# The skip weights of the Mamba layer: one load of a table of 128 rows in place of two loads by single elements

## The chip, the cores and the metric

The kernel runs on one core of a Trainium2 chip. A core has a matrix engine (TensorE, PE in the profile; PEld is its loading of weights), three engines for elementwise work (VectorE or DVE, ScalarE or ACT, GpSimd or POOL), and SyncE (SP), which here only issues transfers. Sixteen DMA engines carry the transfers between the device memory (HBM) and the on-chip memory (SBUF, 128 partitions); PSUM takes the results of matrix products. The engines work side by side and wait for each other by semaphores. The metric is device time in microseconds of one execution; less is better. Outputs must agree with the reference.

## The reference

Two layers on 1024 latent tokens and 256 context tokens of width 1024: a Mamba layer (state space, both directions of time), then attention, each with a modulated norm before and a gate behind. Cut to what matters here:

```
for i in range(2):
    sh, scl, gt = split(silu(c) @ mod_w[i] + mod_b[i], 3)      # the same with c_ctx for the context tokens
    in_lat = rmsnorm(h_lat, norm_w[i]) * (1 + scl) + sh
    ...
# the Mamba layer
z, xbc, dt = split(h @ in_w);  xbc = silu(conv5(xbc) + conv_b)
xs, B, C = split(xbc);         dt = softplus(dt + dt_bias)
y = scan_forward(xs, dt, B, C) + scan_backward(...)            # 32 heads of 64 channels
y = y + dsk * xs                                               # dsk: one skip weight for each of the 32 heads
out = rmsnorm(y * silu(z), norm_w) @ out_w
```

The skip weights are the input m_d, 32 numbers. Shift and scale of the first layer come from the product of silu(c) and silu(c_ctx) with the first 2048 columns of mod_w[0].

## The kernel before, in words

Everything is float32; large products are made from a high and a low part of each operand, three matrix instructions per product (the helper mm3, lines 167 to 170).

**Who decides the order.** The kernel first makes a list of operations, each with an engine, a duration that was written in by hand, a rank, the operations it comes after and the buffers it takes. The class Plan then walks through these in a small event loop of its own (method order, lines 82 to 131). For each engine that is free it takes the operation of lowest rank whose predecessors are done and whose buffers are free. The result is one fixed order per engine, and the instructions are written in it. Transfers are operations of "SP": each keeps SP for 0.38 units of the list's time, and those made by the helper small (line 280) count as 0.05 of transfer time, the 256 KB pieces as 0.9. These are numbers of the list, not of the chip. The chip then runs each engine's instructions in that order, each as soon as its semaphores allow.

**The head.** Before the first large product the kernel does the following.

- It loads the 10 token tiles of 128 x 1024 (function normalised, line 339 for the load, 512 KB each, ranks from -1000 to -851). ScalarE squares and sums a tile, VectorE and GpSimd form the inverse root, VectorE scales the tile (line 353).
- It computes shift and scale of the first layer (function sums, lines 283 to 330). mod_w[0] comes in 32 pieces of 128 x 512 (256 KB, line 297, ranks -900 to -869) into a buffer named spare that holds 20 of them; a piece waits until the product twenty pieces earlier is done. Each piece is multiplied with cc, the 16 columns of silu(c) and silu(c_ctx) (line 303; two matrix instructions for each piece). Pieces 0 to 7 add into the PSUM tile st, 8 to 15 into yo, and the last sixteen into two yd tiles. ScalarE copies each sum out (mrow, line 313), TensorE turns it (line 319), and VectorE makes the columns shcol and gcol (lines 223 to 326).
- Function modulated (lines 356 to 379) turns the scaled tiles on TensorE, applies scale and shift (raw, lines 371 and 373) and splits them into the two parts inh and inl. All later products of the Mamba layer read these.
- Seven small loads are listed under the name rest (lines 397 to 400), with ranks -850 to -844: convw, convb, dtbias, a_bc, mnw, and two for dskip. Their sizes in SBUF are 128 x 160, 128 x 32, 64 x 1, 128 x 64, 128 x 16 and, for dskip, two times 64 x 16. (modbc of 128 x 32 and normw and cc of 128 x 16 are loaded at the start.)
- w_dt (256 KB, line 423) and the first halves of the projection weights w_in (256 KB each, line 606) follow with ranks of -30 and above, through two raw buffers (wraw). ScalarE makes their high part (lines 431 and 611), VectorE or GpSimd the low part (lines 434 and 614).

All these loads are issued by SP, on one queue, in the order of the list.

**The skip weights.** dskip is a tile of 128 partitions x 16 (line 248). Column j belongs to channel tile j of 128 channels, that is two heads: partitions 0 to 63 hold the weight of head 2j, partitions 64 to 127 that of head 2j + 1. m_d lies in HBM as 32 numbers in a row. Each of the two loads fills 64 partitions: all 64 read the same 16 numbers, every second one of m_d, from the first or the second on. The tile is read at line 822 alone, where VectorE adds skip weight times xs to the result of the scan.

**Behind the head** come the projections with their convolutions (lines 622 to 675), the scan by groups of heads (mix, from line 677), the gated norm and the output product, and the attention layer. TensorE's products set their pace.

Of the kernel before, what the change touches and what calls it, by code (L numbers as in the profile page):

```python
# [137 lines left out]
def rows(ap, parts):  # L138
    return bass.AP(tensor=ap.tensor, offset=ap.offset, ap=[[0, parts]] + [list(d) for d in ap.ap])
# [6 lines left out]
def emit(tc, A, out):  # L146
# [7 lines left out]
    def scratch(name, shape):  # L154
        return DR.tile(shape, FT, name=name)
# [8 lines left out]
    m_d = scratch("m_d", [2, 4096])  # L164
# [40 lines left out]
    convw = P0.tile([128, 32, 5], FT, name="convw")  # L205
    convb = P0.tile([128, 32], FT, name="convb")
    mnw = P0.tile([128, 16], FT, name="mnw")
# [40 lines left out]
    dskip = SM.tile([128, 16], FT, name="dskip")  # L248
    dtb = SM.tile([128, 1], FT, name="dtbias")
    dtbias = dtb[64:128]  # L250
    a_bc = SM.tile([128, 64], FT, name="a_bc")
# [28 lines left out]
    def small(rank, dst, src):  # L280
        return plan.op("SP", lambda: Q.dma_start(dst, src), [], rank, small=True)
# [112 lines left out]
    for b in range(3):  # L394
        modulated(b, xs[(0, 2, 6)[b]:(2, 6, 10)[b]], cols, -800 + 100 * b)

    rest = [small(-850 + i, *p) for i, p in enumerate(
        [(convw, A["conv_w"]), (convb, A["conv_b"]), (dtbias, A["dt_bias"]), (a_bc, rows(A["a_log"], 128)), (mnw, A["m_norm_w"])] +
        [(dskip[j * 64:(j + 1) * 64], bass.AP(tensor=A["m_d"].tensor, offset=A["m_d"].offset + j, ap=[[0, 64], [2, 16]]))
         for j in range(2)])]  # L400


    second = [plan.op("-", change("su2", reuse_waits="tile"), list(ready_in.values()), us=0.)]
# [1456 lines left out]
def layout(inp):  # L1860
    import numpy as np
    f=lambda n: np.asarray(inp[n])
    d = {}
    d['x']=f('x')[0]; d['ctx']=f('ctx')[0]
    cols=lambda v: v.reshape(-1,128).T
    d['cc']=np.stack([cols(f('c')[0]), cols(f('c_ctx'))],-1)
    d['norm_w']=np.stack([cols(f('norm_w')[i]) for i in range(2)],1)
    d['mod_w']=f('mod_w'); d['mod_b']=f('mod_b')
    d['mod_bc']=np.stack([cols(f('mod_b')[i][:2048]) for i in range(2)],1)
    d['final_norm_w']=f('final_norm_w')  # L1870
    w=f('m_in_w')[0]
    d['w_in']=w[:,:6144].reshape(8,128,48,128).transpose(2,1,0,3).reshape(48,128,1024)
    d['w_dt']=w[:,6144:].reshape(8,128,64).transpose(1,0,2).reshape(128,512)
    d['conv_w']=f('m_conv_w')[0].reshape(5,32,128).transpose(2,1,0)
    d['conv_b']=cols(f('m_conv_b')[0])
    d['a_log']=f('m_a_log')[0].reshape(64); d['dt_bias']=f('m_dt_bias')[0].reshape(64,1)
    d['m_d']=f('m_d')[0]
    d['m_norm_w']=cols(f('m_norm_w')[0])
    d['m_out_w']=f('m_out_w')[0]
    a=f('a_in_w')[0]  # L1880
    tile4=lambda w: w.reshape(8,128,512).transpose(1,0,2).reshape(128,4096)
    d['wqkv']=np.stack([tile4(a[:,j*512:(j+1)*512]) for j in range(3)])
    d['wg']=a[:,1536:].reshape(8,128,8,128).transpose(2,1,0,3).reshape(8,128,1024)
    d['a_out_w']=f('a_out_w')[0]
    d['q_norm']=f('a_q_norm')[0]; d['k_norm']=f('a_k_norm')[0]
    r,c=np.meshgrid(np.arange(16),np.arange(64),indexing='ij')
    inv=(np.float32(10000.0)**(-np.arange(0,32,2,dtype=np.float32)/np.float32(32))).astype(np.float32)
    ar=r.reshape(-1).astype(np.float32)[:,None]*inv; ac=c.reshape(-1).astype(np.float32)[:,None]*inv

    ang=np.stack([ar,ac],1)  # L1890
    cs=np.cos(ang); sn=np.sin(ang)
    cos=np.stack([cs,cs],2).reshape(1024,64); sin=np.stack([-sn,sn],2).reshape(1024,64)
    d['rope']=np.stack([cos,sin],1).reshape(8,128,2,64).transpose(1,0,2,3)
    return {k:np.ascontiguousarray(v,dtype=np.float32) for k,v in d.items()}
# [17 lines left out]
```

## Time and profile before

| | us |
|---|---|
| time, median of 3 runs | 1996.26 |
| lowest and highest | 1993.16, 1997.48 |
| profiled execution: span from first to last instruction | 1992.2 |
| TensorE busy in that span | 1923.3 (97%) |
| VectorE, ScalarE, GpSimd busy | 1450.7, 1114.1, 1199.4 |
| mean granted clock of TensorE | 0.989 of full speed |

For the profiled execution only the span is given, no time of its own beside it. Durations and starts are in microseconds from the span's start unless a row says ns. A row of a timeline gives start, duration, engine, line, operation, output<-inputs, shapes and count; brackets give the idle time just before it and who ended it. SPq is the issuing of a transfer by SP. The timeline merges neighbours of one kind, so that "x5" may contain waits. A row of waits gives who waited for whom: total, times, longest. The DMA share is a mean over the sixteen engines, and can come out a few per cent above 1.

### The profile page before, as it was taken

To read this page: it belongs to the slowest core of one execution; us is meant where nothing else is said; L and a number is where in the kernel's file an instruction comes from. 1 tells how busy PE (TensorE), PEld (TensorE's weight loads), DVE (VectorE), ACT (ScalarE), POOL (GpSimd) and SP (SyncE) were. 2 spreads that over 40 slices of the span, in tenths; PEclk is the share of its full clock that TensorE was granted. 3 is DMA by queue.
4 is the path that set the end of the run, shared out by engine and by line. 5 is a ranking of instruction groups with operands and counts; after the bars stand their busy time and mean duration, and the time that the engine had idled before them with its cause. 6 is when DMAs were issued, how large, how long until landed. Compare 5 with 4: busy or idle time off the path is not lost.

```text
span 1992.2 us, 30263 instructions
## 1 busy us (share of the span) xinstructions
PE 1923.3 (97%) x10552; PEld 1448.4 (73%) x10552; DVE 1450.7 (73%) x1734; ACT 1114.1 (56%) x2046; POOL 1199.4 (60%) x973
## 2 busy tenths in 40 slices
PE   5799999999999999999999999999999999999998
PEld 1578888888888888888878878877775444444476
DVE  1585887887969796867545898768675888888643
ACT  2537768666667777677644775533224454444521
POOL 1212766676757585768379788764355677776722
PEclk8899999999999999999999999999999999999999
DMA  6114463635363545356586675552232011110033
GB/s 246 64 32 131 129 187 115 186 104 174 115 190 104 149 137 175 121 151 175 162 278 206 224 253 187 165 152 93 77 109 83 32 39 48 48 46 24 9 104 106
DMA packets 162125, 255.48 MB, mean 128 GB/s; under 512 B 21466, under 2 KB 57178, under 8 KB 161972
## 3 DMA queue, kind: packets, MB, share of 16 engines
q1 hardware_dynamic: 160820, 251.71, 41.1%
q8 instruction: 83, 1.36, 0.3%
q10 hardware_dynamic: 1152, 1.84, 0.3%
q14 instruction: 70, 0.57, 0.1%
HBM read 210.78 MB, written 42.63 MB: 127 GB/s over the span
## 4 chain that ended last, share of the span: by engine, by line
PE 85%; DVE 6%; DMA 2%; issue 2%; ACT 2%; POOL 2%; SPq 1%; DVEq 0%; POOLq 0%; ACTq 0%
PE pj L168 10%; PE pj L169 10%; PE pj L170 10%; PE sc L1675 7%; PE ot L1691 7%; PE ob L168 7%; PE ob L170 6%; PE ob L169 6%; PE yo L849 3%; PE st L730 3%; PE sc L1474 2%; DVE acc L657 2%; PE yd L807 2%; PE sc L168 2%; PE sc L170 2%
## 5 line engine op out<-in xcount | busy, mean ns | idle before, releaser
L168 PE MATMUL pj<-inh,whi 128*128 128x512 f32 (+1 forms) x1152 | 442.0, 384 | 5.1 <-DVE dv L465 3.2
L169 PE MATMUL pj<-inl,whi 128*128 128x512 f32 (+1 forms) x1152 | 410.1, 356 | 0.8 <-POOL inl L379 0.8
L170 PE MATMUL pj<-inh,wlo 128*128 128x512 f32 (+1 forms) x1152 | 410.4, 356 | 0.0
L168 PEld LDWEIGHTS pj<-inh,whi 128*128 128x128 f32 x1152 | 219.1, 190 | 34.4 <-DVE dv L465 3.6
L170 PEld LDWEIGHTS pj<-inh,wlo 128*128 128x128 f32 x1152 | 218.2, 189 | 32.1
L169 PEld LDWEIGHTS pj<-inl,whi 128*128 128x128 f32 x1152 | 219.3, 190 | 26.9 <-POOL inl L379 1.2
L657 DVE SCALAR_TENSOR_TENSOR acc<-ub,convw,acc 128x1282 f32<-128x1282 f32 x128 | 229.2, 1791 | 10.5 <-ACT acc L654 6.4
L766 POOL TENSOR_SCALAR_AFFINE_SELECT lab<-lab 128x512 f32<-128x512 f32 x160 | 148.6, 934 | 143.0 <-DMA lab<-la_d 117.6
L772 ACT ACTIVATE W<-lab,u_t 128x128 f32<-128x128 f32 x640 | 203.4, 391 | 51.6 <-POOL lab L766 23.0
L1656 POOL TENSOR_TENSOR acc<-acc,P 128x1024 f32<-128x1024 f32 x80 | 192.5, 2406 | 64.5 <-ACT P L1680 62.9
L1680 ACT ACTIVATE P<-sc 128x1024 f32<-128x1024 f32 x160 | 162.7, 1025 | 115.7 <-PE sc L1675 106.0
L1621 DVE TENSOR_REDUCE mx<-sc 128x2 f32<-128x1024 f32 (+1 forms) x140 | 167.4, 1214 | 38.6 <-PE sc L1474 37.6
L725 POOL TENSOR_TENSOR xw<-xst,te_t 128x256 f32<-128x256 f32 x144 | 145.9, 1026 | 27.6 <-PE st L730 17.8
L1691 PE MATMUL ot<-P,vv 128*64 128x512 f32 x640 | 154.7, 605 | 0.0
L614 POOL TENSOR_TENSOR wlo<-wraw,whi 128x512 fp32r<-128x512 f32 x48 | 70.9, 1477 | 122.8 <-ACT whi L611 119.1
L1675 PE MATMUL sc<-q,kh 64*128 64x512 f32 x640 | 135.9, 420 | 0.5 <-ACT P L1680 0.2
L785 DVE TENSOR_TENSOR W<-W 128x512 f32<-128x512 f32 x80 | 81.8, 1023 | 47.4 <-ACT W L772 42.4
L170 PE MATMUL ob<-whi,yl 128*128 128x512 f32 x288 | 113.4, 394 | 1.9 <-DVE yl L1073 1.4
L168 PE MATMUL ob<-whi,yh 128*128 128x512 f32 x288 | 113.9, 395 | 0.0
L169 PE MATMUL ob<-wlo,yh 128*128 128x512 f32 x288 | 112.9, 392 | 0.0
L1675 PEld LDWEIGHTS sc<-q,kh 64*128 64x128 f32 x640 | 60.0, 184 | 69.8 <-DVE mx L1621 29.6
L744 POOL TENSOR_TENSOR tm<-PV,dec_t 128x512 f32<-128x512 f32 x64 | 89.2, 1393 | 35.2 <-DVE PV L748 34.4
(285 smaller groups left out, 4446.1 us busy)
## 6 DMA issues: line engine op xcount, KB each, us to landing
lab<-la_d SPq DMA_DIRECT2D x160, 256.0 KB
wraw<-in_w_in SPq DMA_DIRECT2D x96, 256.0 KB
workvv<-in_m_out_w SPq DMA_DIRECT2D x94, 256.0 KB
mraw<-in_mod_w SPq DMA_DIRECT2D x64, 256.0 KB
es<-e_d SPq DMA_DIRECT2D x128, 128.0 KB
wraw<-in_wqkv SPq DMA_DIRECT2D x48, 256.0 KB
spare<-in_mod_w SPq DMA_DIRECT2D x32, 256.0 KB
q_d<-qs SPq DMA_DIRECT2D x64, 128.0 KB
```

What stands on the lines that cost most here:

```text
L168: T.matmul(o, lh, rh, start=first, stop=False)
L169: T.matmul(o, lh, rl, start=False, stop=False)
L170: T.matmul(o, ll, rh, start=False, stop=last)
L657: V.scalar_tensor_tensor(t["a"], ub[i % 2][:, k:k + CW], convw[:, ct, k:k + 1], t["a"], op0=OP.mult, op1=OP.add)
L725: G.tensor_tensor(t[d], s["xst"][:, c], te_t[:, d, c, h4][:, :, None].to_broadcast([128, 4, 64]), op=OP.mult)
L766: G.affine_select(t["l", d], t["l", d], [[0, 4], [sgn, 128]], OP.is_ge, NEVER, base=0, channel_multiplier=-sgn)
L772: S.activation(t["w", d][:, h], t["l", d][:, h], AF.Exp, bias=u_t[:, d, c, 4 * g + h:4 * g + h + 1])
L1621: V.tensor_reduce(max_place(t["m"][0], i), o, AX.X, OP.max)
L1656: E.tensor_tensor(t[e], t["P", k0] if two else t[e], t["P", kt], op=OP.add)
L1675: T.matmul(o[:, h], (first_row[r] if n == 3 else (kh, kl, kh)[n][r, kv, k]), x[(0, 0, 1, 2)[n]][r], start=(n == 0), stop=(n == 3))
L1680: S.activation(t["P", kt], flat(t["s", kt]), AF.Exp)
L1691: T.matmul(t["o"][h * 64:(h + 1) * 64], vv[:, kt, kv], t["P", kt][:, h * 512:(h + 1) * 512], start=(kt == 0), stop=(kt == NT - 1))
```

## The change

The host lays the skip weights out as the tile needs them: 128 rows of 16 numbers, each weight repeated over its 64 rows. The two entries for dskip in the list become one, a plain load of 128 x 16, of the same shape as mnw ahead of it. It has rank -845, which the first of the two had; rank -844 is gone, so the list has one SP operation fewer. Nothing else in the kernel is edited; the order is worked out anew from the list.

```
     rest = [small(-850 + i, *p) for i, p in enumerate(
-        [(convw, A["conv_w"]), (convb, A["conv_b"]), (dtbias, A["dt_bias"]), (a_bc, rows(A["a_log"], 128)), (mnw, A["m_norm_w"])] +
-        [(dskip[j * 64:(j + 1) * 64], bass.AP(tensor=A["m_d"].tensor, offset=A["m_d"].offset + j, ap=[[0, 64], [2, 16]]))
-         for j in range(2)])]
+        [(convw, A["conv_w"]), (convb, A["conv_b"]), (dtbias, A["dt_bias"]), (a_bc, rows(A["a_log"], 128)), (mnw, A["m_norm_w"]),
+         (dskip, A["m_d"])])]
...
-    d['m_d']=f('m_d')[0]
+    d['m_d']=np.repeat(f('m_d')[0].reshape(16,2).T,64,axis=0)
```

The function small is `plan.op("SP", lambda: Q.dma_start(dst, src), [], rank, small=True)`; layout, which holds the last two lines, runs on the host before the launch.

## The prediction

> **What bounds the kernel now.** I read the page first: the busy shares, then the slices, to find where TensorE isn't busy.
>
> ```profile
> span 1992.2 us, 30263 instructions
> PE 1923.3 (97%) x10552; PEld 1448.4 (73%) x10552; DVE 1450.7 (73%) x1734; ACT 1114.1 (56%) x2046; POOL 1199.4 (60%) x973
> PE   5799999999999999999999999999999999999998
> ```
>
> TensorE is busy 97% of the span, so for nearly all of it only TensorE's own work counts. The idle 68.9 us (1992.2 - 1923.3) are not spread evenly: only the first two slices (about 100 us) show a 5 and a 7. A change to a transfer of 4 KB can matter only there, since its data are first used at 215.5 us (the first issue of line 822, the only reader of the skip weights). The view of busy time by stretches cuts this head; its columns are the stretch, its length, the busy time of PE, PEld, DVE, ACT and POOL, then the granted clock, the DMA share and GB/s:
>
> ```profile
> core 0: us, PE busy (x) PEld busy (x) DVE busy (x) ACT busy (x) POOL busy (x), PEclk, DMA share, GB/s
> 5.00:35.00 30.00, 25.57 (x66) 5.32 (x66) 7.23 (x17) 11.88 (x21) 4.51 (x9) 1.00 1.04 392
> 36.00:53.00 17.00, 0.87 (x2) 0.00 (x0) 1.59 (x3) 0.33 (x2) 0.95 (x1) 0.61 0.05 1
> 53.00:60.00 7.00, 3.29 (x4) 0.30 (x5) 0.76 (x2) 1.29 (x3) 1.26 (x1) 0.50 0.83 300
> 120.00:1992.00 1872.00, 1841.46 (x10212) 1402.25 (x10210) 1402.17 (x1663) 1064.41 (x1964) 1177.50 (x936) 1.00 0.42 128
> L822 DVE SCALAR_TENSOR_TENSOR acc<-acc,dskip,yd x48: 467/735/750, 215.5 to 981.4; 128x512 f32<-128x512 f32 x32, 128x256 f32<-128x256 f32 x16
> ```
>
> Until 35 us the DMA engines move 392 GB/s. From 36 to 53 us, 17 us, they move 1 GB/s, and no engine does anything. At 53 us the stream returns. What they do in the gap is told by the transfer view, of the first 130 us and of 36 to 53 us:
>
> ```profile
> DMA packets 10806, 16.77 MB, mean 129 GB/s; under 512 B 3888, under 2 KB 4016, under 8 KB 10800
> ...
> DMA packets 1792, 0.01 MB, mean 1 GB/s; under 512 B 1790, under 2 KB 1790, under 8 KB 1792
> ```
>
> In the gap 1790 packets passed, nearly all under 512 bytes, with only 0.01 MB. The order of SP's issues is in its timeline (start, duration, issue):
>
> ```profile
> 26.63 0.33 SPq L297 DMA_DIRECT2D spare<-in_mod_w  x1
> 27.26 0.33 SPq L339 DMA_DIRECT2D xt<-in_x  x1
> 27.99 0.33 SPq L297 DMA_DIRECT2D spare<-in_mod_w  x1
> 28.61 0.33 SPq L281 DMA_DIRECT2D convb<-in_conv_b  x1
> 29.88 0.58 SPq L281 DMA_DIRECT2D dtbias<-in_dt_bias  x1
> 31.18 0.34 SPq L281 DMA_DIRECT2D a_bc<-in_a_log  x1
> 31.85 0.33 SPq L281 DMA_DIRECT2D mnw<-in_m_norm_w  x1
> 33.14 1.40 SPq L281 DMA_DIRECT2D dskip<-in_m_d  x2
> 35.14 2.81 SPq L297 DMA_DIRECT2D spare<-in_mod_w  x1
> 38.00 6.42 SPq L423 DMA_DIRECT2D wraw<-in_w_dt  x1
> 44.47 3.14 SPq L606 DMA_DIRECT2D wraw<-in_w_in  x1
> 47.71 8.53 SPq L297 DMA_DIRECT2D spare<-in_mod_w  x5
> ```
>
> The two dskip loads write 2 x 64 partitions x 16 elements, and the source steps by two elements, so each element travels alone: 2048 pieces of 4 bytes. The count bears that out: of the 3888 small packets in 130 us, the other small loads (cc, normw, modbc, convb, a_bc, mnw with 128 rows each, dtbias with 64) explain 832, and 63 transfers with 16 closing packets each, if each has so many, 1008; that leaves 2048. In the gap they pass one after another: 1790 in 17 us is 105 in a us, 9.5 ns each. Behind them stand, in SP's order, piece 26 of the modulation weights (the load into "spare", pieces counted from 0), w_dt, the first w_in and pieces 27 to 31: the issues that took 0.33 us now take 2.81, 6.42 and 3.14 us. And the chain of waits runs through exactly these:
>
> ```profile
> 36.89 1.07 SPq L297
> 38.00 6.42 SPq L423
> 44.47 3.14 SPq L606
> 47.71 10.83 DMA spare<-in_mod_w
> 58.58 5.30 PE yd L303 x10
> ```
>
> The 32 products of line 303 with these pieces give shift and scale of the first layer, and every normalised tile waits for them. So the 17 us lie wholly on the path that sets the end.
>
> **The change, part by part.** *Removed:* 2048 elements at 9.5 ns, 19.5 us of the queue, and two issues (1.40 us of SP). *Added:* one load of 128 rows of 64 bytes, the shape of mnw's and of cc's load. For cc there is an end to read, on an idle queue: issued at 0.81 us, read by ScalarE at 2.43 us:
>
> ```profile
> 0.81 0.40 SPq L211 DMA_DIRECT2D cc<-in_cc  x1
> 2.43 0.21 ACT L213 ACTIVATE cc<-cc 128x16 f32<-128x16 f32 x1 [0.35 <-DMA cc<-in_cc]
> 35.00:36.00 1.00, 0.15 (x1) 0.09 (x2) 0.00 (x0) 0.82 (x1) 0.44 (x1) 1.00 0.49 75
> ```
>
> For the queue the bounds of the new load are 0.02 us (8 KB at 392 GB/s) and 1.2 us (128 packets at the elements' 9.5 ns). I take 0.2 us: the rows ahead of it passed quickly too, within the 35 to 36 us slice. One issue of 0.33 us takes the place of 1.40 us.
>
> A rule of the Trainium skill speaks against the gain. Its page "DMA: Bandwidth & Descriptors", section "Why a DMA increments its semaphore by 16 and not by 1", has a transfer spread over up to 16 engines when the outermost sizes divide by 16, as 64 does here. The trace shows a mean share of 0.05 of 16 engines, 0.8 of one, so whatever the spread, the elements aren't moved side by side; what follows if they were is a rival below. The same page, "Rules for kernel authors", says that a strided last dimension becomes one descriptor per element, and that agrees with the count of 2048.
>
> *Moved:* everything behind dskip in SP's queue. The host's repetition of the weights runs before the launch and costs the device nothing. The planner has one SP entry fewer, so SP may be free before the slot of piece 26 is, and w_dt may go ahead of piece 26. Either way the same eight loads of 256 KB stand ahead of the last product, so the sum doesn't depend on it.
>
> Now the new times. The earlier stream ends at about 35.2 us (392 GB/s up to 35, then 75 GB/s on average in the slice to 36). The small rows then still in the queue, with the new dskip, I put at 0.7 us: the slice 35 to 36 holds them and elements together, so 1.0 is the upper end and 0 the lower. Eight loads of 262,144 bytes at 392 GB/s take 5.35 us, 0.67 us each. A piece's product starts about 0.6 us after its bytes: piece 25's starts at 35.85 us, the stream before it ends at 35.2.
>
> ```profile
> 27.55 5.35 PE L303 MATMUL yd<-spare,cc 128*2 128x512 f32 x12
> ...
> 35.85 1.02 PE L303 MATMUL yd<-spare,cc 128*2 128x512 f32 x2 [0.92 <-DMA spare<-in_mod_w]
> 56.55 1.87 PE L303 MATMUL yd<-spare,cc 128*2 128x512 f32 x2 [19.67 <-DMA spare<-in_mod_w]
> 58.58 5.29 PE L303 MATMUL yd<-spare,cc 128*2 128x512 f32 x10 [0.17 <-DMA spare<-in_mod_w]
> ```
>
> So piece 31 is ready at 35.2 + 0.7 + 5.35 + 0.6 = 41.9 us and piece 27 four loads earlier, at 39.2 us. TensorE takes longer per piece than the transfers: twelve instructions took 5.35 us at full clock where pieces were waiting, two to a piece, 0.89 us each. Five pieces from 39.2 us end at 39.2 + 4.4 = 43.6 us. Before, that end is 58.58 + 5.29 = 63.9 us. **Gain: 63.9 - 43.6 = 20.3 us.** It holds more than the 17 us of the gap, since the slow return of the stream (300 GB/s in 53 to 60 us) and the half clock (0.50 there) go too.
>
> The bounds. *Least:* SP's entries could follow at the widest spacing of the undisturbed rows, 1.3 us (28.61, 29.88, 31.18). Eight entries after 33.5 us put the last issue at 43.9 us; with 2.3 us to landing (cc's 1.62 and 0.67 for its bytes) and 0.9 of product the end is 47.1 us, and the gain 16.8 us. *Most:* nothing in between, 35.2 + 5.35 + 0.6 + 0.9 = 42.0 us, a gain of 21.9 us. If the clock is down again, five pieces take the 5.3 us of before, not 4.4, and 19.4 us are gained. I take 20.3 us because the entries at 26.63, 27.26 and 27.99 us were 0.68 us apart under a full stream, which is the pace of the bytes.
>
> What is late next? The x tiles are scaled by 38.4 us, and the two first w_in halves are split at 63.3 us while their first products start at 68.0 us:
>
> ```profile
> 37.64 0.75 DVE L353 TENSOR_SCALAR xt<-xt,rsq 128x1024 f32<-128x1024 f32 x1 [0.44 <-POOL rsq L352]
> 57.66 0.76 DVE L434 TENSOR_TENSOR wd<-wraw,wd 128x256 fp32r<-128x256 f32 x2 [19.27 <-ACT wd L431]
> 62.57 0.69 DVE L614 TENSOR_TENSOR wlo<-wraw,whi 128x512 fp32r<-128x512 f32 x1 [4.15 <-ACT whi L611]
> 68.03 0.56 PE L168 MATMUL pj<-inh,whi 128*128 128x256 f32 x1
> ```
>
> The x tiles have 5 us in hand before 43.6 us. The second w_in half needs w_dt's buffer, free once w_dt is split (0.76 us on VectorE, and ScalarE's part before it); w_dt lands five transfers or more ahead of piece 31, so the half goes out right behind piece 31. It lands 0.67 us after that, at 42.6 us, and is split some 1.4 us later (0.69 us on VectorE, about as much on ScalarE before), at 44.0 us, against a first use at 68.0 - 20.3 = 47.7 us. So both covers stay, and what follows moves up as a whole. After 120 us TensorE idles 1872.0 - 1841.5 = 30.5 us in all, for waits on data that move along with it.
>
> The sum is made against one execution with a span of 1992.2 us. Its time outside the span isn't shown; the median of the runs, 1996.26 us, stands 4.1 us above the span, and I leave that unchanged. 1996.26 - 20.3 = **1976.0 us**.
>
> **The rivals.** *One: the elements are not the cause.* If the packets went side by side over 16 engines, 2048 of them at the 7.6 ns that a share of 0.05 gives (0.05 x 16 x 17 us / 1792) would be through in 2048 x 7.6 / 16 = 1.0 us. Something else would then have stopped the stream, and the gain would be about 1 us: 1995 us. That is what the spreading rule of the Trainium skill quoted above would make of it. Against it: the count of 2048, and that the seven issues shown ahead of the dskip pair took 0.33 to 0.58 us and those behind it up to 6.42. 5%.
>
> *Two: part is given back.* With an entry gone the planner may order the later work differently, or a cover above may be thinner than worked out. The longest wait of TensorE behind this stage is 3.2 us; three new ones of that size take 9.6 us: 20.3 - 9.6 = 10.7, 1985.6 us. For it: the order comes from due times, and one entry less shifts them. Against it: nearly all later work hangs on the same pieces, so its due times move together. 12%.
>
> ```profile
> PE pj L168 <- DVE dv L465: 3.2, 1, 3.2
> ```
>
> *Three: slower.* If a different order of the planner let TensorE run dry in the long projection stage, the loss would have to exceed 20.3 us before the kernel gets slower, two thirds of the 30.5 us that it idles in the whole rest. Doubling that idle time gives 1996.26 - 20.3 + 30.5 = 2006.5 us. For it speaks only that the order is recomputed; against it, that the buffers and the ranks of all later entries stay the same. 3%.
>
> *Four: the change doesn't do what it says,* because rows of 64 bytes feed as slowly as elements. At 9.5 ns that is 1.2 us, a gain of 19.3 us: inside the forecast.
>
> **How the numbers follow.** The forecast has 80%, with its own range 1972 to 1982 us: the gains 16.8 to 21.9 give 1974.4 to 1979.5, and the runs before scatter by about 2.2 us to a side. I widen to 1970 to 1985 us, for a little more gain from order and half of rival two; outside lie rivals one and three, 8%, and the other half of two with stray cases, about 8 more. Faster by over 0.2% (4.0 us, about what a measurement can tell from no change) is the forecast, and rival two: 92%. Within 0.2% is rival one: 5%. Slower: 3%.
>
> **What would show it.** Right: two dskip issues become one of about 0.33 us, packets under 512 B fall by about 1,900 (2048 less 128), the stretch 36 to 41 us carries about 390 GB/s, the products of line 303 end near 43.6 us and the wait of 19.67 us for "spare" is under 3; the first modulated tile starts near 45 us, and busy time after that stays. Wrong: the gap is still there or has moved behind another small load (dtbias has 64 single elements); or it is gone, but the first w_in product doesn't start near 48 us; or the span from there to the end has grown.

## The result, and the profile after

The changed kernel takes 1981.32 us (median of 4 runs, 1978.23 to 1984.47), beside 1996.87 us (1993.16 to 1998.08) of the kernel before on the same chip. The ratio is 0.9926, with a 95% interval of 0.9911 to 0.9941: 15.55 us less. The forecast was 1976.0 us with a range of 1970 to 1985.

The profiled execution of the changed kernel is its slowest, 1984.47 us, 1.8 us of it outside the span. So the two spans, 1992.2 and 1982.7 us, differ by 9.5 us only, though the medians differ by 15.5; single events are compared below by when they happen, and the gain by medians. The page of the changed kernel, its busy shares and TensorE's slices:

```profile
span 1982.7 us, 30262 instructions
PE 1927.6 (97%) x10552; PEld 1450.6 (73%) x10552; DVE 1448.0 (73%) x1734; ACT 1113.9 (56%) x2046; POOL 1202.0 (61%) x973
PE   7899999999999999999999999999999999999998
```

The 5 and the 7 at the head have become a 7 and an 8; nothing else has moved. The changed kernel's busy time by stretches (columns as in the prediction: PE, PEld, DVE, ACT, POOL, then granted clock, DMA share, GB/s):

```profile
5.00:35.00 30.00, 24.86 (x65) 5.15 (x66) 7.06 (x16) 11.64 (x20) 4.40 (x8) 1.00 1.03 391
36.00:41.00 5.00, 2.51 (x4) 0.17 (x4) 2.26 (x5) 2.38 (x5) 1.50 (x3) 0.82 0.82 242
42.00:44.00 2.00, 1.95 (x3) 0.34 (x4) 0.00 (x0) 0.00 (x0) 0.00 (x0) 0.50 1.03 386
44.00:46.00 2.00, 2.00 (x3) 0.25 (x2) 0.00 (x0) 0.63 (x1) 0.00 (x0) 0.50 0.42 159
46.00:48.00 2.00, 2.00 (x6) 0.34 (x4) 0.69 (x1) 0.00 (x1) 0.00 (x0) 0.98 0.19 24
120.00:1982.70 1862.70, 1829.29 (x10139) 1391.41 (x10137) 1388.43 (x1653) 1059.92 (x1958) 1177.37 (x935) 1.00 0.43 128
```

The 17 us at 1 GB/s are gone. But the stream does not go on at its old pace: 242 GB/s in 36 to 41 us where 391 ran before, and TensorE is at half clock until 46 us. The transfer view of the first 130 us, SP's timeline, and the timeline of TensorE and ScalarE, all of the changed kernel:

```profile
DMA packets 9015, 17.05 MB, mean 131 GB/s; under 512 B 1968, under 2 KB 2096, under 8 KB 9008
```

```profile
28.66 0.33 SPq L297 DMA_DIRECT2D spare<-in_mod_w  x1
29.30 0.33 SPq L281 DMA_DIRECT2D convb<-in_conv_b  x1
30.57 0.57 SPq L281 DMA_DIRECT2D dtbias<-in_dt_bias  x1
31.86 0.33 SPq L281 DMA_DIRECT2D a_bc<-in_a_log  x1
32.53 0.33 SPq L281 DMA_DIRECT2D mnw<-in_m_norm_w  x1
33.81 0.33 SPq L281 DMA_DIRECT2D dskip<-in_m_d  x1
34.48 0.33 SPq L422 DMA_DIRECT2D wraw<-in_w_dt  x1
35.85 0.33 SPq L297 DMA_DIRECT2D spare<-in_mod_w  x1
36.53 0.33 SPq L605 DMA_DIRECT2D wraw<-in_w_in  x1
36.95 2.27 SPq L297 DMA_DIRECT2D spare<-in_mod_w  x5
```

```profile
36.55 1.02 PE L303 MATMUL yd<-spare,cc 128*2 128x512 f32 x2 [0.94 <-DMA spare<-in_mod_w]
38.82 1.49 PE L303 MATMUL yd<-spare,cc 128*2 128x512 f32 x2 [1.24 <-DMA spare<-in_mod_w]
42.05 6.43 PE L303 MATMUL yd<-spare,cc 128*2 128x512 f32 x10 [1.75 <-DMA spare<-in_mod_w]
48.52 0.59 ACT L313 ACTIVATE mrow<-yd 2x512 f32<-2x512 f32 x1 [2.52 <-PE yd L303]
```

Packets under 512 bytes fall from 3888 to 1968, 1920 fewer: 2048 less 128, as forecast. The dskip load is issued in 0.33 us and so are those right behind it. TensorE's longest wait for "spare" falls from 19.67 to 1.75 us. Pieces 27 to 31, the last ten instructions, run from 42.05 to 48.5 us; before, from 58.58 to 63.9. The copy of their sums to "mrow", with which everything downstream begins, I use as the mark of the head: 63.9 before, 48.5 after, 15.4 us earlier, and the medians differ by 15.5.

Do the later stages move along? The waits of the changed kernel's TensorE in 36 to 120 us, and the line of its skip weights' reader, line 821 now:

```profile
PE yd L303 <- DMA spare<-in_mod_w: 3.9, 3, 1.8
PE pj L168 <- DVE dv L464: 2.6, 1, 2.6
```

```profile
L821 DVE SCALAR_TENSOR_TENSOR acc<-acc,dskip,yd x48: 467/735/749, 201.6 to 970.6; 128x512 f32<-128x512 f32 x32, 128x256 f32<-128x256 f32 x16
```

The first use of the skip weights comes 13.9 us earlier (215.5 to 201.6), the last 10.8 (981.4 to 970.6), the end of the span 9.5. No new wait appears: the old one for the tile dv (line 465 before, 464 now) is 2.6 us where it was 3.2. After 120 us TensorE idles 1862.7 - 1829.3 = 33.4 us, 30.5 before, and its busy time in the whole span is 4.3 us longer with the same 10552 instructions. This loss belongs to the pair of executions, not to the kernels, as far as the medians tell.

### The profile page after: what moved, and what is told of

Read it like the earlier page. It is cut to its first block, busy times and chain, and to the rows that moved or that the text cites. A ratio compares the mean times of both kernels' runs of the same rounds, so it can differ in the third digit from the quotient of the medians.

```text
span 1982.7 us, 30262 instructions
## 1 busy us (share of the span) xinstructions
PE 1927.6 (97%) x10552; PEld 1450.6 (73%) x10552; DVE 1448.0 (73%) x1734; ACT 1113.9 (56%) x2046; POOL 1202.0 (61%) x973
## 4 chain that ended last, share of the span: by engine, by line
PE 84%; DVE 7%; DMA 3%; ACT 2%; issue 2%; POOL 2%; SPq 0%; DVEq 0%; POOLq 0%; ACTq 0%
PE pj L168 9%; PE pj L170 9%; PE pj L169 9%; PE sc L1674 7%; PE ot L1690 7%; PE ob L168 7%; PE ob L170 6%; PE ob L169 6%; PE yo L848 3%; PE st L729 3%; PE sc L1473 2%; DVE acc L656 2%; PE yd L806 2%; PE sc L168 2%; PE sc L170 1%
## 5 line engine op out<-in xcount | busy, mean ns | idle before, releaser
L724 POOL TENSOR_TENSOR xw<-xst,te_t 128x256 f32<-128x256 f32 x144 | 147.2, 1035 | 30.6 <-PE st L729 19.2
L1674 PEld LDWEIGHTS sc<-q,kh 64*128 64x128 f32 x640 | 59.9, 184 | 69.8 <-DVE mx L1620 29.5
L913 DVE SCALAR_TENSOR_TENSOR macc<-mraw,cc,macc 128x512 f32<-128x512 f32 x98 | 101.2, 1052 | 12.5 <-DMA mraw<-in_mod_w 12.3
```

The lines of the kernel that those rows point to most:

```text
L724: G.tensor_tensor(t[d], s["xst"][:, c], te_t[:, d, c, h4][:, :, None].to_broadcast([128, 4, 64]), op=OP.mult)
L1674: T.matmul(o[:, h], (first_row[r] if n == 3 else (kh, kl, kh)[n][r, kv, k]), x[(0, 0, 1, 2)[n]][r], start=(n == 0), stop=(n == 3))
```

## The experiments

All edits are to the changed kernel unless the text says "before". The kernel before took 1996.24 (median) beside the first four, 1997.2 beside the next four, 1995.6 beside the last four. The labels of the theories are those of the expectations: the single elements hold the queue (A), the number or order of the issues does it (B), the source pattern with step zero does it (C), reads of the same few bytes wait for each other (D), two loads of 64 partitions do it (E).

**The order of the issues.** SP has one entry less, and w_dt now goes out ahead of piece 26. An empty SP entry gives the order of before back:

```diff
          (dskip, A["m_d"])])]
+    plan.op("SP", lambda: None, [], -844, small=True)
```

> The changed kernel (one load of 128 rows) with an empty SP entry in the list in place of the second dskip load, so that the list has as many entries as before and w_dt stands behind piece 26 again. Theory A (the single elements hold SP's queue): as the changed kernel, the last sum is copied out (mrow, the last of four) at 48.5 us give or take 2.5, ratio 0.990 to 0.995. Theory B (the gain is the SP entry that is gone and the order that follows): as the kernel before, mrow at about 64 us, ratio 0.998 to 1.002.

1983.0 us (1977.18 to 1984.61), ratio 0.9929 [0.9914, 0.9944]; "mrow" at 49.4. The gain is all there with the old order.

**Two loads again, by rows.** The host's table, in two loads of 64 rows of 64 bytes:

```diff
+        [(dskip[j * 64:(j + 1) * 64], A["m_d"][j * 64:(j + 1) * 64]) for j in range(2)])]
```

> Two loads again, but of rows: the host's table of 128 x 16, loaded as two halves of 64 rows of 64 bytes. Theory A (single elements): no gap in the stream, mrow at 48.5 us give or take 2.5, ratio 0.990 to 0.995. Theory B (two transfers instead of one): mrow at about 64 us, ratio about 1.

1983.84 us (1979.03 to 1986.77), ratio 0.9942 [0.9928, 0.9955]; "mrow" at 49.5. Two issues instead of one cost nothing that shows. With the first experiment, B falls.

**One load, but by single elements.** The host's table turned round, so that each of the 2048 numbers is again a piece of its own:

```diff
-         (dskip, A["m_d"])])]
+         (dskip, bass.AP(tensor=A["m_d"].tensor, offset=A["m_d"].offset, ap=[[1, 128], [128, 16]]))])]
...
-    d['m_d']=np.repeat(f('m_d')[0].reshape(16,2).T,64,axis=0)
+    d['m_d']=np.repeat(f('m_d')[0].reshape(16,2),64,axis=1)
```

> One load, but by single elements: the host lays the table out transposed, 16 x 128, and the one load of 128 partitions x 16 reads every 128th number, 2048 elements of 4 bytes. Theory A (single elements): the gap is back, 1700 to 1900 small packets in 17 us without bulk data, mrow at 62 to 66 us, ratio 0.998 to 1.002. Theory B (two transfers instead of one): as the changed kernel, mrow at 48.5 us, ratio 0.9925.

This should have brought the stop back, by my theory. It didn't: 1980.93 us (1974.83 to 1982.66), ratio 0.9918 [0.9903, 0.9934], "mrow" at 48.5. The transfer view of this kernel, 35 to 38 us and 37 to 39 us:

```profile
DMA packets 2574, 0.33 MB, mean 111 GB/s; under 512 B 2435, under 2 KB 2435, under 8 KB 2574
...
DMA packets 338, 0.63 MB, mean 313 GB/s; under 512 B 32, under 2 KB 32, under 8 KB 338
```

The 2048 elements are there, and are over by about 37 us: of 2435 small packets in 35 to 38 us at most 32 come after 37, so at least 2403 pass in 2 us, 1200 a us, the last rows of the small loads ahead among them. Before it was 105 a us. **Theory A falls**: single elements alone do not hold the queue. What differs from before is where they are read from. Before, all come from the same 128 bytes (32 numbers); here from 8 KB.

**Another queue.** The two loads of before with their source, in place of the one load, from ScalarE's queue, once the seventh x tile is scaled:

```diff
+    for j in range(2):
+        plan.op("ACT", lambda j=j: S.dma_start(dskip[j * 64:(j + 1) * 64], bass.AP(
+            tensor=A["m_d"].tensor, offset=A["m_d"].offset + j, ap=[[0, 64], [2, 16]])), [xs[6][2]], -844)
```

> The two loads by single elements as before, but issued by ScalarE on its own queue, once x tile 6 is scaled (about 33 us). It asks where the elements stand in the way. If in SP's queue: SP's stream goes on beside them, mrow at 48 to 52 us, ratio 0.990 to 0.996, with about 2000 small packets spread under the bulk data. If in something that all queues share (the making of packets, or the engines): the stream stops as before, mrow at 62 to 66 us, ratio about 1.

1995.42 us (1991.73 to 1998.03), ratio 0.9995 [0.9986, 1.0003]: nothing gained. SP is not held up any more in issuing the pieces, in this kernel's timeline of issues:

```profile
35.38 2.94 SPq L297 DMA_DIRECT2D spare<-in_mod_w  x6
37.17 1.42 ACTq L400 DMA_DIRECT2D dskip<-in_m_d  x2
```

Its transfer view by queues, 46 to 54 us (q10 is ScalarE's, q1 SP's; packets, MB, share of 16 engines):

```profile
q10 hardware_dynamic: 863, 0.00, 4.7%
q1 hardware_dynamic: 19, 0.03, 1.3%
```

In 8 us 863 elements pass, 108 a us as before, and SP's queue gets 0.03 MB, though its pieces have all been issued by 38.3 us. The last piece is multiplied at 49.4 us only, and ScalarE, which now has the first half of w_in ahead of the copy to "mrow", waits for it until 61.5, in its timeline:

```profile
61.48 0.63 ACT L612 ACTIVATE whi<-wraw 128x512 fp32r<-128x512 f32 x1 [20.48 <-DMA wraw<-in_w_in]
62.01 0.57 ACT L313 ACTIVATE mrow<-yd 2x512 f32<-2x512 f32 x1
```

So the stop is shared: it isn't a matter of standing behind the elements in one queue.

**Two loads of 64 partitions by elements, source spread out:**

```diff
+        [(dskip[j * 64:(j + 1) * 64], bass.AP(tensor=A["m_d"].tensor, offset=A["m_d"].offset + 1024 * j, ap=[[1, 64], [64, 16]]))
+         for j in range(2)])]
...
-    d['m_d']=np.repeat(f('m_d')[0].reshape(16,2).T,64,axis=0)
+    d['m_d']=np.repeat(f('m_d')[0].reshape(16,2).T[:,:,None],64,axis=2)
```

> Two loads of 64 partitions by single elements as in the kernel before, 2048 elements, but each partition reads numbers of its own (the host lays out 2 x 16 x 64; the step from partition to partition is one number in place of none). Theory C (the step of zero in the partition dimension makes the elements go single file) and theory D (all reads fall on the same 128 bytes): no long gap, the last mrow at 46 to 52 us. Theory E (two loads of 64 partitions): the gap is back, mrow at 62 to 66 us.

1983.04 us (one run), "mrow" at 49.2: no stop. The shape of before, two loads over 64 partitions by elements, is harmless when each has bytes of its own. E falls.

**One load over 128 partitions, source as before.** The kernel before, with the two loads made one; the odd heads then get the even heads' weights:

```diff
+         (dskip, bass.AP(tensor=A["m_d"].tensor, offset=A["m_d"].offset, ap=[[0, 128], [2, 16]]))])]
```

> One load over 128 partitions, 16 elements each with a source step of two, and the step from partition to partition zero: 2048 elements like the kernel with the transposed table, the zero step being the difference. Heads with odd numbers get the skip weights of even ones. Theories C and D: the gap is back, about 105 small packets in a us for 19 us, mrow at 62 to 66 us. Theory E: no gap, mrow at 46 to 52 us.

1993.9 us (one run). Its TensorE timeline and its transfer view of 37 to 39 us:

```profile
57.22 6.99 PE L303 MATMUL yd<-spare,cc 128*2 128x512 f32 x12 [19.46 <-DMA spare<-in_mod_w]
```

```profile
DMA packets 213, 0.00 MB, mean 0 GB/s; under 512 B 213, under 2 KB 213, under 8 KB 213
```

The stop is back in full, with one load: a wait of 19.46 us (19.67 before), 213 packets in 2 us. It goes with the source.

**Near bytes without a step of zero.** The kernel before, one load whose partitions each start one number further on, over 632 bytes (the numbers repeated five times); most heads then get another head's weight:

```diff
+         (dskip, bass.AP(tensor=A["m_d"].tensor, offset=A["m_d"].offset, ap=[[1, 128], [2, 16]]))])]
...
-    d['m_d']=f('m_d')[0]
+    d['m_d']=np.resize(f('m_d')[0],160)
```

> One load over 128 partitions, source step two within a partition and one from partition to partition, so all 2048 elements come from 632 bytes that are read many times, but no step is zero. The skip weights are wrong for most heads. Theory C (zero step): no gap, mrow at 46 to 52 us. Theory D (the same few bytes): single file again, 62 to 66 us, or something in between.

1989.85 us (one run). Its TensorE timeline, and its transfers in 37 to 39 us:

```profile
47.56 7.88 PE L303 MATMUL yd<-spare,cc 128*2 128x512 f32 x12 [10.64 <-DMA spare<-in_mod_w]
```

```profile
DMA packets 416, 0.00 MB, mean 1 GB/s; under 512 B 416, under 2 KB 416, under 8 KB 416
```

Half the stop: 208 packets a us, 4.8 ns each, twice the rate of before. No step is zero here, so a stop without it is against C and for D; and a source some five times as wide gives twice the rate, not five times.

**A step of zero over far bytes.** The two loads of before with their step of zero; only the host puts the 32 numbers 512 bytes apart:

```diff
-        [(dskip[j * 64:(j + 1) * 64], bass.AP(tensor=A["m_d"].tensor, offset=A["m_d"].offset + j, ap=[[0, 64], [2, 16]]))
+        [(dskip[j * 64:(j + 1) * 64], bass.AP(tensor=A["m_d"].tensor, offset=A["m_d"].offset + 128 * j, ap=[[0, 64], [256, 16]]))
...
-    d['m_d']=f('m_d')[0]
+    d['m_d']=np.repeat(f('m_d')[0],128)
```

> The two loads of the kernel before with their step of zero from partition to partition and 16 single elements per partition, the only difference being that the host spaces the 32 numbers 512 bytes apart (a table of 16 KB), so that the 2048 reads fall on 32 places in memory, 64 on each. Theory C (the zero step itself): single file, mrow at 62 to 66 us. Theory D (reads of the same few bytes wait for each other): several at a time, no gap over 3 us, mrow at 46 to 52 us.

1979.11 us (one run), "mrow" at 49.6. Its transfers in 35 to 38 us:

```profile
DMA packets 2552, 0.32 MB, mean 106 GB/s; under 512 B 2418, under 2 KB 2418, under 8 KB 2552
```

This is the sharpest of the runs: two loads, the same partitions, the same 2048 elements, each number still read 64 times, the same step of zero; the distance between the numbers alone is changed, and the stop is gone. So C falls, and D has to be put more exactly: it is not that one number is read often, but that the reads lie close together in memory. How close is not settled. In every run with a stop the neighbouring numbers of a partition lie 8 bytes apart, in the three runs by elements without one 256, 512 or 1024 bytes, so the step within a partition and the width of the table changed together. Only the runs over 128 and over 632 bytes have the same step, and their rates differ, so the step alone does not set the rate.

**Half the dose.** The kernel before; the even heads' 64 partitions by elements as there, the odd heads' by rows of 64 bytes:

```diff
+        [(dskip[j * 64:(j + 1) * 64], (bass.AP(tensor=A["m_d"].tensor, offset=A["m_d"].offset, ap=[[0, 64], [2, 16]]), A["m_dr"])[j])
...
+    d['m_d']=f('m_d')[0]; d['m_dr']=np.repeat(f('m_d')[0][None,1::2],64,axis=0)
```

> Half the dose: the even heads' 64 partitions are loaded as before (1024 single elements of the same bytes), the odd heads' 64 partitions as rows of 64 bytes from a table of the host. If each element costs 9.5 ns of the queue and nothing else matters: a gap of about 9 us in place of 17, and mrow halfway between 48.5 and 63.9, at 54 to 58 us. If the stop doesn't scale with the number (a fixed cost of such a load, or of the second one): mrow near 48.5 or near 64.

1990.01 us (one run); its TensorE timeline:

```profile
47.89 7.59 PE L303 MATMUL yd<-spare,cc 128*2 128x512 f32 x12 [10.72 <-DMA spare<-in_mod_w]
```

The wait is 10.72 us instead of 19.67: 1024 x 9.5 ns = 9.7 us of elements. The stop goes by the number of reads; it lands where the run over 632 bytes does (2048 x 4.8 ns = 9.8 us).

**Where the missing 4.8 us went.** Forecast were 20.3 us, measured 15.5. In the changed kernel w_dt and the first half of w_in go out ahead of pieces 27 to 31. Here both wait until piece 31 has gone out:

```diff
-            a = plan.op("SP", bring, first, -900 + i, takes=[hp])
+            a = X["in"] = plan.op("SP", bring, first, -900 + i, takes=[hp])
...
-        a = plan.op("SP", bring, [], DT_RANK - 40, takes=[raw])
+        a = plan.op("SP", bring, [X["in"]], DT_RANK - 40, takes=[raw])
...
-        a = plan.op("SP", bring, after, rank - 40, takes=[raw])
+        a = plan.op("SP", bring, [*after, X["in"]], rank - 40, takes=[raw])
```

> The changed kernel (20 slots), with w_dt and the first w_in half put behind piece 31 in SP's queue. The slow packets of 36 to 42 us in the changed kernel's trace begin with these two. If they are what holds up pieces 27 to 31: mrow at 43 to 46 us in place of 48.5, ratio 0.989 to 0.9915. If the pieces are slow themselves: mrow at 47.5 to 50 us, ratio 0.992 to 0.994.

1975.35 us (1973.31 to 1978.52), ratio 0.9899 [0.9884, 0.9914]: 20.2 us. Its timeline and its stretches:

```profile
41.03 2.74 PE L303 MATMUL yd<-spare,cc 128*2 128x512 f32 x6 [0.43 <-DMA spare<-in_mod_w]
43.80 0.59 ACT L313 ACTIVATE mrow<-yd 2x512 f32<-2x512 f32 x1 [6.96 <-PE yd L303]
```

```profile
36.00:41.00 5.00, 3.92 (x8) 0.42 (x8) 1.59 (x3) 0.84 (x2) 0.94 (x1) 1.00 0.86 267
```

The end of the products is at 43.8 us, where 43.6 was forecast for the changed kernel. Of the 4.7 us between 48.5 and 43.8, about 2.1 are the two loads that no longer stand ahead (0.52 MB at some 250 GB/s), and 2.0 are the clock, which stays at 1.00 (ten instructions in 6.43 us in the changed kernel, against 5 x 0.89 = 4.4). The pace of the stream is not better: 267 GB/s. So the slow stream itself remains.

**All 32 pieces ahead of the small loads.** Thirty-two slots for pieces instead of twenty (the rest in a buffer that is free so early), so that no piece waits for a slot:

```diff
-    plan = Plan({"piece": 20, "xt": 4, ...
+    plan = Plan({"piece": 32, "xt": 4, ...
...
+                if i in (0, 20):
+                    X["spare", i // 20] = BIG.tile([128, KT * TOK], FT, tag=("inh", "inl")[i // 20], name=("spare", "spareb")[i // 20])
+                w = X["spare", i // 20][:, (i % 20) * 512:(i % 20 + 1) * 512]
```

> The changed kernel with 32 slots for the pieces of the modulation weights in place of 20 (the buffer of the low part, idle then, takes twelve), so that SP issues all pieces ahead of the last four x tiles, the small loads, w_dt and w_in. If the 5 us by which the change fell short come from what still stands ahead of pieces 26 to 31 in the queue: mrow at 35 to 40 us in place of 48.5, ratio to the kernel before 0.985 to 0.990. If the pieces are late for another reason (slow packets wherever they are): mrow at 44 to 49 us, ratio about 0.992. If the x tiles, now later, become the bound: mrow early and the ratio still 0.990 to 0.993.

1979.82 us (1977.47 to 1981.29), ratio 0.9914 [0.9897, 0.993]. "mrow" is copied at 41.0 us, a little behind the 35 to 40 of the expectation's first case and 7.5 earlier than in the changed kernel, and little of that reaches the end (17.4 us gained against the kernel before beside it, where the changed kernel gained 15.5). This kernel's waits of TensorE in 36 to 120 us say why, and its stretch:

```profile
PE tc L366 <- DVE raw L373: 5.9, 3, 3.0
```

```profile
36.00:41.00 5.00, 4.95 (x12) 0.85 (x10) 0.00 (x0) 0.02 (x1) 0.00 (x0) 1.00 1.03 360
```

The pieces have taken the place of the x tiles: VectorE does nothing in 36 to 41 us, where it is busy 2.26 us in the changed kernel, with x tiles and w_dt, and TensorE then waits for modulated tiles. The cover that the prediction gave 5 us in hand is used up here.

**The same, with the x tiles between the pieces.** In addition all x tiles get ranks three apart, as tiles 2 to 5 had:

```diff
-    xs = [normalised(t, -1000 + t if t < 2 else -900 + (6 + 3 * (t - 2) if t < 6 else 40 + t)) for t in range(10)]
+    xs = [normalised(t, -1000 + t if t < 2 else -900 + 6 + 3 * (t - 2)) for t in range(10)]
```

> The kernel with 32 slots, and the last four x tiles ranked between the pieces (every third piece, as the first four are) in place of behind them. If in the kernel with 32 slots the late x tiles took back what the early pieces gave: mrow at 41 to 43 us, TensorE's waits on scaled tiles (L366) back from 7 to under 4 us, and ratio to the kernel before 0.986 to 0.990, faster than both. If the head behind mrow is bound by VectorE and ScalarE anyway: ratio 0.991 to 0.993.

1972.54 us (1970.65 to 1973.59), ratio 0.9882 [0.9865, 0.9898]: the fastest here, 23.1 us under the 1995.6 beside it. This kernel's waits, timeline and stretch:

```profile
PE tc L366 <- DVE raw L373: 2.4, 2, 2.2
```

```profile
34.84 7.33 PE L303 MATMUL yd<-spareb,cc 128*2 128x512 f32 x16
42.21 0.59 ACT L313 ACTIVATE mrow<-yd 2x512 f32<-2x512 f32 x1
```

```profile
36.00:39.00 3.00, 2.86 (x7) 0.42 (x6) 0.91 (x2) 1.15 (x2) 0.79 (x2) 1.00 1.04 383
```

The products run without a wait, at full clock, from pieces that come at 383 GB/s; the small loads come behind them, and the wait for modulated tiles shrinks from 5.9 to 2.4 us.

All runs together, by when "mrow" is copied:

| kernel | reads of dskip | "mrow", us | time, us |
|---|---|---|---|
| one load over 128 partitions, 128 bytes | 2048 elements | 64.2 | 1993.9 |
| before | 2048 elements, 128 bytes | 63.9 | 1996.3 |
| on ScalarE's queue | 2048 elements, 128 bytes | 62.0 | 1995.4 |
| half the dose | 1024 elements, 128 bytes | 55.5 | 1990.0 |
| near bytes, no step of zero | 2048 elements, 632 bytes | 55.5 | 1989.9 |
| numbers 512 bytes apart | 2048 elements, 16 KB | 49.6 | 1979.1 |
| two loads by rows | 128 rows | 49.5 | 1983.8 |
| old order | 128 rows | 49.4 | 1983.0 |
| two loads by elements, spread | 2048 elements, 8 KB | 49.2 | 1983.0 |
| after | 128 rows | 48.5 | 1981.3 |
| one load by elements, spread | 2048 elements, 8 KB | 48.5 | 1980.9 |
| w_dt and w_in behind the pieces | 128 rows | 43.8 | 1975.4 |
| pieces first, x tiles between | 128 rows | 42.2 | 1972.5 |
| pieces first, x tiles late | 128 rows | 41.0 | 1979.8 |

Within 3 us or so the time follows the head one for one; the last row leaves the line, by the wait on line 373.

## Why the prediction was right, and where it wasn't

**The place and the price: right.** The stop lay on the path to the end, it was the dskip pair that made it, and it cost 9.5 ns for each read. Removing it moved the head 15.4 us and the end with it. Half as many reads gave half the stop. (That no engine does anything from 36 to 53 us is not quite what the prediction's own row says: TensorE is busy for 0.87 us of it, VectorE for 1.59.)

**The cause: half right.** The prediction said that 2048 single elements pass one after another, 9.5 ns each. The count was right (1920 packets fewer), and so was the rate; but that they were single was not the reason. Elements just as single pass at over 1000 a us when they are read from 8 or 16 KB; out of 632 bytes the rate is 208 a us, out of 128 bytes 105. The step that failed is the one from "one after another" to "because each travels alone": no row of the trace of before spoke for it, since only this one source had elements in such numbers. The changed kernel does two things at once: far fewer reads, and a table in memory in which nothing is read twice. The spread alone is enough, as three runs show; fewer reads out of the same 128 bytes alone were run only down to 1024.

"One after another" doesn't hold either. The trace has the start of every packet. In the run with one load over 128 partitions, 37 to 49 us, the sixteenth element behind each one starts 149 to 152 ns after it in over nine of ten cases (in the kernel before the median is 151 ns), and about a third of the elements start within the 7 ns that the record ahead of them lasts. So sixteen streams go side by side, each with one element in 150 ns: 2048 / 16 x 150 ns = 19.2 us, about the wait of 19.67. Out of 632 bytes 32 elements pass in 151 ns. Sixteen engines that are each busy for 7 ns of 150 give just the share of 0.05 from which the prediction concluded that the elements aren't moved side by side. That each stream is one engine fits this, but the records don't name the engine.

So the first rival had the premise and not the conclusion. It said that elements side by side would be through in 1.0 us; spread out, they nearly are, 2403 small packets in 2 us. The Trainium skill's rule that it rested on ("DMA: Bandwidth & Descriptors", section "Why a DMA increments its semaphore by 16 and not by 1": the outermost sizes set over how many engines a transfer goes) agrees with the sixteen streams, if each is an engine. It does not tell how long an engine takes for an element: the rival worked out 7.6 ns from the share, and the trace shows 150. To conclude that the elements could then not be the cause was wrong.

**The size: 15.5 us instead of 20.3.** The mis-sized term is the one of the eight 256 KB loads: "Eight loads of 262,144 bytes at 392 GB/s take 5.35 us", and "either way the same eight loads of 256 KB stand ahead of the last product, so the sum doesn't depend on it". The stream ran at 242 GB/s. The prediction took its pace from issues 0.68 us apart under a full stream, and SP's rows above have only one 256 KB load, w_dt, in the 7 us between the issues of two pieces (28.66 and 35.85); more on this under "Open". With it the two steps that hung on it fell: piece 27 was ready at 42.05 us, not 39.2, and TensorE, going from piece to piece with gaps of 0.9 to 1.8 us, dropped to half clock, so that five pieces took 6.43 us, not 4.4. Together 2.9 + 2.0 = 4.9 us: 48.5 against 43.6. The prediction's own remark on the clock ("five pieces take the 5.3 us of before") put 0.9 us on it; but before, the clock came back at about 60.3 us, 1.7 us into those 5.3, and now at about 46, 4 us into 6.4. That the order does not matter was wrong too: with the two loads behind the pieces, 20.2 us were gained. The sum's own bounds, a head that ends between 42.0 and 47.1 us and a gain of 16.8 to 21.9, do not hold the measured 48.5 and 15.5; they had no case in which late pieces and a low clock come together. The stated range held because it had been widened for other reasons, the scatter of the runs and half of the second rival, and that is luck.

**What followed: right.** Both covers held: the x tiles were scaled in time, and the first w_in product started at 52.5 us, 15.5 earlier than the 68.0 of before, though not at the 48 of the forecast. The first modulated tile starts at 50.1, not near 45, late by nearly the same 4.9 us. Three of the prediction's signs of being right thus failed (390 GB/s from 36 to 41 us, the end of the products near 43.6, the first modulated tile near 45), and one of its signs of being wrong came (no w_in product near 48). The second rival, part given back by another order, is not what happened: on all engines the order is that of before but for two places, w_dt ahead of piece 26 on SP, and the scaling of the last x tile behind w_dt's split on VectorE; and with SP's old order the time is the same. The third rival's longer idle time in the later stages didn't come. The fourth, 64-byte rows as slow as elements, is out too: 128 of them cannot be seen in the stream.

**Time outside the span.** The prediction added the 4.1 us between the median and one span. For the changed kernel's profile 1.8 us lie outside the span. The 4.1 was thus mostly the distance of that execution from the median. The sum of a gain and a median doesn't suffer from it.

**Open.** Why reads of nearby bytes take longer, and how wide the piece of memory is within which they do: only 128 and 632 bytes, and 8 and 16 KB, were run. Whether an element waits for those of other streams: on ScalarE's queue the last few streams, 59.9 to 60.4 us, repeat every 75 ns, so 150 is not a stream's fixed time. Why bulk packets of another queue don't pass in between.

And why the stream from 36 to 41 us is slow: 236, 251, 242 and 267 GB/s in the four runs in which rows of dskip stand ahead of the last pieces, whatever the order, and 360 to 383 in the two with the pieces ahead of all small loads. The traces show a part of it. SP's waits in the changed kernel, 28 to 37 us:

```profile
SPq L281 <- DMA xt<-in_x: 2.6, 3, 0.9
```

In this trace's first 37 us, wherever an issue of SP is released by a transfer (28 times), it is by the landing of the load eight places ahead: a_bc's issue at 31.86 waits for the x tile issued at 25.23, w_in's at 36.53 for the piece issued at 28.66. So a small load takes one of eight places from a large one. With five small loads in a row the large ones run low, and from 36 to 40 us the DMA engines are busy to a share of 0.74 to 0.84, where it was 1.03. This can't be all: the eight loads are all issued by 39.3 us, and 40 to 42 us still carries only 269 GB/s. No run changed the small loads alone, so the cause isn't shown.

## What to carry to other kernels

Where the DMA share falls to 0.05 and nothing moves, look at the source addresses, not only at the size of the pieces: a small table that was broadcast out of 128 bytes by single elements took 9.5 ns for each read and stopped SP's loads, from SP's queue and from ScalarE's. Laying the table out in full on the host costs no device time, and spreading its numbers apart did as much here. A low share does not mean that only one engine works: here it was sixteen streams, each waiting for most of the time. And count what stands between the small loads and the last transfer of a chain: moving two loads of 256 KB behind it was worth another 4.7 us (20.2 against 15.5), nearly a third of the cure itself.

## What the runs showed of the hardware that I had not expected

- 4-byte reads from the same 128 bytes go at 105 a us (16 side by side, each 150 ns), from 632 bytes at 208, from 8 to 16 KB at over 1000. Two loads over 64 partitions or one over 128 made no difference that shows, nor did a step of zero where the numbers lay apart.
- Such reads on ScalarE's queue leave SP's bulk stream 0.03 MB in 8 us.
- The clock fell to 0.50 although TensorE worked for half of the time. The stretches of the changed kernel, and of the one with w_dt and w_in behind the pieces:

```profile
36.00:38.00 2.00, 1.02 (x2) 0.09 (x2) 0.84 (x2) 1.21 (x3) 0.76 (x2) 1.00 0.74 237
38.00:40.00 2.00, 1.18 (x2) 0.09 (x2) 1.43 (x3) 0.68 (x3) 0.31 (x1) 0.81 0.84 246
```

```profile
36.00:38.00 2.00, 1.43 (x3) 0.17 (x4) 0.84 (x2) 0.84 (x2) 0.83 (x1) 1.00 0.75 241
38.00:40.00 2.00, 1.89 (x5) 0.25 (x4) 0.75 (x1) 0.00 (x0) 0.11 (x1) 1.00 0.92 261
```

In the first TensorE is busy 2.2 of 4 us, with no pause over 1.3 us, and the clock goes down; in the second it is busy 3.3 of 4 us, and it stays at 1.00. In the first it came back at about 46 us, 4 us after the products ran without a pause.
